# An expert stage's weights, gathers and order of work rewritten in a hybrid decoder layer

## The chip, the cores and the metric

The kernel runs on one core of one Trainium2 chip. The metric is the device time of one execution in microseconds (us), as the median of several runs. The engines are named as the profile names them: PE (TensorE, with PEld for its weight loads), DVE (VectorE), ACT (ScalarE), POOL (GpSimd) and SP (SyncE). Several engines can start DMAs, and all DMAs share the core's 16 DMA engines.

## The reference

One decoder layer over 4096 tokens of 1024 channels. A first sub-layer mixes tokens in four head groups and projects the result; the change doesn't touch its arithmetic. The second sub-layer is a mixture of 64 experts. Each token picks one group of eight experts and two experts in it.

```
hid = silu(xb @ w_gate[e]) * (xb @ w_up[e])     # xb: rows of the tokens of expert e, 1024 channels -> 256
y   = (hid @ w_down[e]) * g[:, None]            # 256 -> 1024, g: the token's gate for this expert
out = out.at[row_tok].add(y)                    # then x = x + gt_f * out, and a last rmsnorm
```

So 8192 pairs of token and expert are spread over 64 experts. With the inputs of the reference the counts by group of eight experts are:

```
 32  37  21  53  29  30  60  38
120 246 115 119 215 391 227 175
 44 147 213 198 114 101  97  82
191  98 206 152 121 138  91 137
 50 257 246 223 110 410 191 169
 62  96  55  58 126  63  26  46
 97  72  89 105 134  89  93  59
118 104 140 114 212 165 141 234
```

Everything is float32. Products use float32r operands, each number split into a high part and a low part, and three products stand for one.

## The kernel before

The layer runs in stages: `first`, `gdn`, `rwkv` (the mixers), `outp` (output projection, second norm, router), `moe` (the experts) and `final` (the last norm). `outp` writes the normed rows to `h2d` in DRAM and the sums to `acc`, and for each expert a list of (token, gate) to `lst`. Entries of a list that nobody takes name one of 128 extra rows past the tokens, with gate zero.

`moe` is one written-out loop over 64 experts. `manual_schedule` keeps each engine's instructions in the order of the program, and the framework adds the semaphores. The parts are:

- `moe_raw` (L1664) starts the loads of an expert's weights on SP into tiles `mraw` of 128x1024 (ten buffers): four tiles of gate|up, each filled by two loads of 256 KB (L1675, runs of 1 KB), and two tiles of down of 512 KB (L1679, runs of 4 KB).
- `moe_split` (L1683) splits a tile: ACT copies the high part (`mgh` or `mdh`, in `act`, L96), and L1688 subtracts it from the raw tile for the low part, on DVE for gate|up (`mgl`), on POOL for down (`mdl`).
- `gather` (L1749) is an indirect DMA on POOL: 128 rows of `h2d` by a list into `mxg`.
- `moe_t` (L1693) transposes 128 gathered rows on PE into PSUM (L1701); ACT and DVE write the two parts `mxh`, `mxl`.
- `moe_g` (L1707): 24 products of 512 columns (L1714 to L1716) give gate|up, then silu on ACT and the product on DVE give `hid`.
- `moe_ht` (L1720) transposes `hid` and splits it into `mhh`, `mhl`.
- `moe_d` (L1731): 12 products (L1741 to L1743), then DVE scales by the gate (L1744) into `my`, and POOL adds the rows to `acc` by an indirect DMA (L1745), which is called the scatter here.
- `count` (L1752) loads an expert's number of tokens into a register of every engine.

A block is 128 rows of one expert. In the loop over e the engines do: gather of the rows of e + 2; splits of gate|up of e + 1 and of down of e; products `moe_g` of e; hidden transposes of e - 1; transposes of the rows of e + 1; `moe_d` of e - 1. Then `If(n > 128)` (L1843) handles e's second block, and in it `If(n > 256)` (L1850) a hardware loop (L1851) over the rest, in which SP loads 128 list entries (`mix`) and POOL gathers the rows (`mxr`). At the end `fetch(e + 2)` starts the weights and, behind its own `If` (L1810), the gather of the second block of e + 2. What is left of an expert's last block (`pend`) is done in the turn of the next expert.

Of the kernel before, what the change touches and what calls it, by code (L numbers as in the profile page):

```python
# [8 lines left out]
F32 = mybir.dt.float32  # L9
# [10 lines left out]
D = 1024  # L20
# [21 lines left out]
class Trunk:  # L42
    """State shared by the stages of the kernel."""

    # when the steps of the two recurrent mixers come, in periods from the start of a superblock
# [17 lines left out]
    def __init__(self, ctx, tc, A, out, S=4096):  # L63
# [7 lines left out]
        # superblocks from which on the short convolution comes at the end of the two recurrent mixers  # L71
# [31 lines left out]
    # ------------------------------------------------------------------ constants  # L103
    def consts(self):
# [4 lines left out]
        def aff(name, shape, fill, keep, tests):  # L109
            """keep where every affine test (pattern, base, channel_multiplier, op) holds, else fill"""  # L110
# [8 lines left out]
        # two diagonal 64-blocks: of ones, and of ones where s <= t of [s, t]  # L119
# [10 lines left out]
    def parts(self, pool, x, bufs):  # L130
        """x [128, 2, 256] in two exact parts"""
# [18 lines left out]
    def col(self, pool, src, n, name):  # L150
        """a vector of n*128 numbers as [128, n] columns"""
# [4 lines left out]
    def row(self, pool, src, n, name):  # L156
        """a vector of n numbers on every partition"""
# [4 lines left out]
    def rsqrt_small(self, pool, x, eps, scale, tag):  # L162
        """(x*scale + eps)^-0.5 of a small tile: exp(-ln/2), then one Newton step"""
# [34 lines left out]
    def ada_step(self, pool, j, k, hp=None):  # L198
        """128 rows of part j of silu(c) @ ada_w, still to be summed over the partitions"""
# [14 lines left out]
    def ada_row(self, pool, psum, j, ptag):  # L214
        """part j of mod as a row in DRAM"""
# [36 lines left out]
    def h_norm(self, pool, t):  # L252
        """rows of tile t over their root mean square"""
# [16 lines left out]
    def h_make(self, pool, hp, psum, ptag, t, xs):  # L270
        """tile t of the modulated norm, channels on partitions, split in two float32r parts"""
# [18 lines left out]
    def h_load(self, hp, t, go=lambda f: f()):  # L290
        """superblock t, [128, TM] for each channel tile; go(f) runs each load"""
# [9 lines left out]
    def h_next(self, hp, t, gen):  # L301
        """the steps of gen; the loads of the superblock after the t-th go between them"""
# [10 lines left out]
    def fill_load(self, i, names, wp, hp, raw):  # L313
        """weights and the first tokens of the short convolution's i-th part"""
# [5 lines left out]
    def h_raw(self, hp):  # L320
        """room for 2048 numbers in the tiles of h_load"""
# [17 lines left out]
    def w_load(self, g, raw, n, src, c0, m=256, o=0):  # L339
        """m columns of src from c0 on to those of a group from o on; raw() is room for n numbers"""  # L340
# [1620 lines left out]
```

## Time and profile before

| | |
|---|---|
| time, median of 3 runs | 4150.07 us (4130.91 to 4164.19) |
| span of the profiled execution | 4143.8 us |
| PE, DVE, ACT, POOL busy, share of the span | 82%, 62%, 42%, 31% |
| DMA moved | 674.87 MB, mean 163 GB/s |
| experts' stage, from the first copy at L1830 on | 2788 to about 4040 us |

The shares are means over stages with different limits. Matmuls are pipelined and their ends are modelled, so a busy PE is not a PE at its peak. The page's DMA share is the mean busy share of the 16 DMA engines; it can pass 1 where packets overlap. PEclk is the granted share of TensorE's full clock.

### The profile page before, as it was taken

The page shows a single profiled execution, that of the slowest core. Times are in us where ns is not written, and L with a number is a line of the kernel's source. Part 1 is how long each engine was busy: PE and PEld are TensorE (multiplying, and loading weights), DVE is VectorE, ACT ScalarE, POOL GpSimd, SP SyncE. Part 2 cuts the span into 40 slices and gives each one's busy share as a digit, 9 for nine tenths or more (in the row PEclk, how much of TensorE's full clock was granted, in tenths as well). Part 3 has the DMA queues.
Part 4 walks back from the last instruction along what each step waited for, and adds up shares of the span by engine and source line. Part 5 has one row for each costly group of instructions (what it writes and reads, how often), then busy time and mean ns, then how long its engine had stood idle before and what let it go on. Part 6 is the DMA issues. An engine that isn't in the chain of part 4 may idle for free. (4 is left out here: it accounts for less than half of the span.)

```text
span 4143.8 us, 75906 instructions
## 1 busy us (share of the span) xinstructions
PE 3410.8 (82%) x28286; PEld 2886.0 (70%) x28286; DVE 2552.2 (62%) x6249; ACT 1740.9 (42%) x3235; POOL 1280.1 (31%) x1256
## 2 busy tenths in 40 slices
PE   5997778899999789999997999958758897588880
PEld 4786667888888678888886877846546675466660
DVE  6455557777776466777753665667535763278654
ACT  4233345655554245555432222226323552145533
POOL 1122221222221123433420112236424663256540
PEclk8999988989999899999998999979979998899995
DMA  8344452232234433333244544349747996489958
GB/s 301 120 174 148 166 169 76 76 99 77 78 96 120 128 93 81 84 106 83 80 126 155 180 139 146 122 147 323 220 143 203 301 284 168 114 267 341 298 151 331
DMA packets 555475, 674.87 MB, mean 163 GB/s; under 512 B 181921, under 2 KB 453561, under 8 KB 554977
## 3 DMA queue, kind: packets, MB, share of 16 engines
q1 hardware_dynamic: 500160, 482.78, 36.5%
q0 software_dynamic: 54816, 185.83, 15.7%
q8 instruction: 267, 4.37, 0.4%
q14 instruction: 232, 1.89, 0.1%
HBM read 487.37 MB, written 181.09 MB: 161 GB/s over the span
## 5 line engine op out<-in xcount | busy, mean ns | idle before, releaser
L1688 DVE TENSOR_TENSOR mgl<-mraw,mgh 128x1024 fp32r<-128x1024 f32 x256 | 403.2, 1616 | 54.3 <-ACT mgh L96 53.1
L1714 PE MATMUL mgu<-mgh,mxh 128*128 128x512 f32 x752 | 313.3, 417 | 92.3 <-PEq L1843 32.4
L96 ACT ACTIVATE mgh<-mraw 128x1024 fp32r<-128x1024 f32 x256 | 258.3, 1049 | 250.2 <-PEq L1843 118.6
L1688 POOL TENSOR_TENSOR mdl<-mraw,mdh 128x1024 fp32r<-128x1024 f32 x128 | 332.0, 2612 | 50.0 <-ACT mdh L96 48.2
L1715 PE MATMUL mgu<-mgl,mxh 128*128 128x512 f32 x752 | 303.3, 403 | 0.0
L1716 PE MATMUL mgu<-mgh,mxl 128*128 128x512 f32 x752 | 302.7, 402 | 0.0
L1714 PEld LDWEIGHTS mgu<-mgh,mxh 128*128 128x128 f32 x752 | 146.0, 194 | 154.0 <-issue 89.5
L1743 PE MATMUL mdn<-mdh,mhl 128*128 128x512 f32 x376 | 166.1, 442 | 77.8 <-DVE mhl L1728 77.8
L1744 DVE SCALAR_TENSOR_TENSOR my<-mdn,mpg,modr 128x512 f32<-128x512 f32 x178 | 133.5, 750 | 97.0 <-PE mdn L1743 95.3
L1741 PE MATMUL mdn<-mdh,mhh 128*128 128x512 f32 x376 | 169.3, 450 | 23.3 <-ACT mhh L96 23.1
L1704 DVE TENSOR_TENSOR mxl<-mtp,mxh 128x512 fp32r<-128x512 f32 x188 | 121.2, 683 | 89.1 <-ACT mxh L96 85.5
L1716 PEld LDWEIGHTS mgu<-mgh,mxl 128*128 128x128 f32 x752 | 145.2, 193 | 36.8 <-DVE mxl L1704 1.6
L1715 PEld LDWEIGHTS mgu<-mgl,mxh 128*128 128x128 f32 x752 | 146.4, 195 | 31.6
L1745 POOL DMA_INDIRECT acc<-my,mpt x64 | 104.9, 1639 | 185.4 <-DVEq L1843 96.6
L1742 PE MATMUL mdn<-mdl,mhh 128*128 128x512 f32 x376 | 160.5, 427 | 1.4 <-POOL mdl L1688 1.4
L82 ACT ACT_TABLE_LOAD x122 | 156.5, 1283 | 3.2 <-PEq L1947 0.8
L1743 PEld LDWEIGHTS mdn<-mdh,mhl 128*128 128x128 f32 x376 | 78.8, 210 | 112.7 <-DVE mhl L1728 92.9
L1749 POOL DMA_INDIRECT mxg<-h2d,ltok x89 | 121.4, 1364 | 113.1 <-DMA acc<-my,mpt 26.1
L1366 POOL TENSOR_TENSOR gSd<-gSb,gcd 128x256 f32<-128x256 f32 x64 | 54.6, 853 | 320.6 <-DVE gSb L1377 301.1
L96 ACT ACTIVATE mxh<-mtp 128x512 fp32r<-128x512 f32 x188 | 102.8, 597 | 102.9 <-PE mtp L1701 102.8
L96 ACT ACTIVATE mdh<-mraw 128x1024 fp32r<-128x1024 f32 x128 | 133.6, 1044 | 0.4 <-ACTq L1850 0.4
L96 ACT ACTIVATE mhid<-mgu 128x256 f32<-128x256 f32 x89 | 33.9, 381 | 231.0 <-PE mgu L1716 230.9
(559 smaller groups left out, 11242.0 us busy)
## 6 DMA issues: line engine op xcount, KB each, us to landing
mraw<-in_moe_w_gate_dram SPq DMA_DIRECT2D x256, 256.0 KB, 6.8
mraw<-in_moe_w_up_dram SPq DMA_DIRECT2D x256, 256.0 KB, 7.0
mraw<-in_moe_w_down_dram SPq DMA_DIRECT2D x128, 512.0 KB, 6.9
hhi<-hs_hi SPq DMA_DIRECT2D x168, 256.0 KB, 4.6
hlo<-hs_lo SPq DMA_DIRECT2D x168, 256.0 KB, 4.9
hx<-in_x_dram SPq DMA_DIRECT2D x32, 512.0 KB, 4.9
hs_hi<-hhi POOLq DMA_DIRECT2D x64, 256.0 KB, 7.4
hs_lo<-hlo POOLq DMA_DIRECT2D x64, 256.0 KB, 7.5
```

The costliest lines, as they stand in the source:

```text
L82: ld = self.nc.scalar.preload_act_table_set(name)
L96: i = self.nc.scalar.activation(out, in_, func, bias=bias, scale=scale, **kw)
L1688: eng.tensor_tensor(lo, raw, hi.bitcast(F32), op=ALU.subtract)
L1704: nc.vector.tensor_tensor(xl[:, s, :], ps, xh[:, s, :].bitcast(F32), op=ALU.subtract)
L1714: nc.tensor.matmul(ps, xh[:, k, :], gh[:, k, :], start=(k == 0), stop=False)
L1715: nc.tensor.matmul(ps, xh[:, k, :], gl[:, k, :], start=False, stop=False)
L1716: nc.tensor.matmul(ps, xl[:, k, :], gh[:, k, :], start=False, stop=(k == KT - 1))
L1741: nc.tensor.matmul(ps, hh[:, f, :], dh[:, f, s], start=(f == 0), stop=False)
L1742: nc.tensor.matmul(ps, hh[:, f, :], dl[:, f, s], start=False, stop=False)
L1743: nc.tensor.matmul(ps, hl[:, f, :], dh[:, f, s], start=False, stop=(f == 1))
L1744: nc.vector.scalar_tensor_tensor(y[:, s], ps, gate, self.gtf[:, s], op0=ALU.mult, op1=ALU.mult)
L1749: self.nc.gpsimd.indirect_dma_start(out=xg, out_offset=None, in_=self.h2d, in_offset=bass.IndirectOffsetOnAxis(ap=tok, axis=0))
```

## The change

Only the experts' stage and what feeds it are changed.

- An expert's 1024 input channels are dealt to partitions as (p k) and no longer as (k p), so that a partition's rows of gate or up lie together: four loads of 512 KB in runs of 4 KB in place of eight of 256 KB. The second norm writes its rows in the matching order of channels (strided write), and the shift row (part 3) and the router's weights are loaded in that order.
- Down of expert e is loaded with gate|up of e + 1.
- Gathers have a bounds check: entries past the tokens are left out, and `h2d` has no extra rows. Tiles that are gathered into are cleared once.
- The lists of all experts are held for 512 entries, token and gate side by side.
- The order of an expert's work: the hidden transposes of e - 1 stand in the middle of `moe_g` of e; the splits of gate|up of e + 1 lie two before and two behind; down's splits come after them, the second one half on POOL and half on DVE.
- The second block's gather (`fetch_more`) is issued for every expert, at the end of the expert before, without an `If`. Blocks 3 and 4 are nested straight code, and the hardware loop is left for more than 512 rows.

```diff
@@ ada_row
-        nc.sync.dma_start(self.modd[j:j + 1], row[0:1])
+        if j == 3:
+            nc.sync.dma_start(self.modd[j:j + 1].rearrange("o (k q) -> o q k", k=KT),
+                              row[0:1].rearrange("o (q k) -> o q k", k=KT))
+        else:
+            nc.sync.dma_start(self.modd[j:j + 1], row[0:1])
...
@@ out_dense
-        V.scalar_tensor_tensor(y, x, r, self.scf, op0=ALU.mult, op1=ALU.mult)
+        swap = lambda a: a.rearrange("p (q k) -> p q k", k=KT)
+        V.scalar_tensor_tensor(y.rearrange("p (k q) -> p q k", k=KT), swap(x), r, swap(self.scf), op0=ALU.mult,
+                               op1=ALU.mult)
...
@@ moe_raw
+        room = lambda: rp.tile([128, 1024], F32, name="mraw", tag="mraw", bufs=10)
+        g, d = [], []
+        if e < 64:
+            for h in range(2):
+                for n in ("moe_w_gate", "moe_w_up"):
+                    g.append(room())
+                    nc.sync.dma_start(g[-1].rearrange("p (k n) -> p k n", k=4),
+                                      A[n][0, e].rearrange("(p k) n -> p k n", p=128)[:, 4 * h:4 * h + 4, :])
+        if e > 0:
+            for f in range(2):
+                d.append(room())
+                nc.sync.dma_start(d[-1], A["moe_w_down"][0, e - 1][f * 128:f * 128 + 128, :])
+        return g, d
...
@@ moe_split_d
+        self.act(hi, raw, AF.Copy)
+        for eng, s in ([(nc.gpsimd, slice(0, D))] if f == 0 else [(nc.gpsimd, slice(0, 512)), (nc.vector, slice(512, D))]):
+            eng.tensor_tensor(lo[:, s], raw[:, s], hi[:, s].bitcast(F32), op=ALU.subtract)
...
@@ moe_g
         for k in range(KT):
+            if mid is not None and k == KT // 2:
+                mid()
...
@@ gather
         self.nc.gpsimd.indirect_dma_start(out=xg, out_offset=None, in_=self.h2d,
-                                          in_offset=bass.IndirectOffsetOnAxis(ap=tok, axis=0))
+                                          in_offset=bass.IndirectOffsetOnAxis(ap=tg[:, 0:1], axis=0),
+                                          bounds_check=self.S - 1, oob_is_err=False)
...
@@ moe
+            more = [pool.tile([128, D], F32, name=f"mxg{i}") for i in range(2)]
...
+            def fetch_more(e):
+                if e < 64:
+                    self.gather(more[0], tg[:, 1, e])
...
+            def turn(pend):
+                return self.moe_ht(pool, psum, pend[0], "mh")
...
                     fetch_x(e + 2)
-                    for k in range(4):
-                        split_g(e + 1, k)
-                        if k % 2:
-                            split_d(e, k // 2)
-                    self.moe_g(psum, wg[e], x, hid)
-                    if pend is not None:
-                        h = self.moe_ht(pool, psum, pend[0], "mh")
-                    x = make_x(e + 1)
+                    split_g(e + 1, 0)
+                    split_g(e + 1, 1)
+                    h = []
+                    ps = self.moe_g(psum, wg[e], x, mid=lambda: h.append(turn(pend)) if pend else None)
+                    split_g(e + 1, 2)
+                    split_g(e + 1, 3)
+                    split_d(e, 0)
+                    self.moe_h(ps, hid)
+                    x = make_x(e + 1)
+                    split_d(e, 1)
+                    n = self.count(ci[0:1, e:e + 1])
                     if pend is not None:
-                        self.moe_d(pool, psum, wd[e - 1], h, pend[1], pend[2], "my", 2)
+                        self.moe_d(pool, psum, wd[e - 1], h[0], pend[1], "my", 2)
                     with tc.If(n > 128):
+                        self.gather(more[1], tg[:, 2, e])
                         h = self.moe_ht(pool, psum, hid, "mi")
-                        x1 = self.moe_t(pool, psum, xgs[e, 1], "mu", 1)
-                        self.moe_d(pool, psum, wd[e], h, tok[:, 0, e:e + 1], pg, "mv", 1)
...
+                        x1 = self.moe_t(pool, psum, more[0], "mu", 1)
+                        self.moe_d(pool, psum, wd[e], h, tg[:, 0, e], "mv", 1)
+                        V.tensor_copy(pt, tg[:, 1, e])
+                        self.moe_h(self.moe_g(psum, wg[e], x1, "igu"), hid)
                         with tc.If(n > 256):
...
+                            self.gather(more[0], tg[:, 3, e])
+                            x1 = self.moe_t(pool, psum, more[1], "mu", 1)
+                            h = self.moe_ht(pool, psum, hid, "mi")
+                            V.tensor_copy(pt, tg[:, 2, e])
+                            self.moe_h(self.moe_g(psum, wg[e], x1), hid)
+                            self.moe_d(pool, psum, wd[e], h, tg[:, 1, e], "mv", 1)
+                            with tc.If(n > 384):
+                                x1 = self.moe_t(pool, psum, more[0], "mu", 1)
+                                h = self.moe_ht(pool, psum, hid, "mi")
+                                V.tensor_copy(pt, tg[:, 3, e])
+                                self.moe_h(self.moe_g(psum, wg[e], x1, "igu"), hid)
+                                self.moe_d(pool, psum, wd[e], h, tg[:, 2, e], "mv", 1)
+                                with tc.If(n > 512):
+                                    with tc.For_i(512, n, 128) as i:
...
+                    fetch_more(e + 1)
                     fetch(e + 2)
```

## Rows read from the trace of the kernel before

**Rows 1.** Windows: start:end, length, then busy us by engine, PEclk, DMA share, GB/s.
```profile
2788.00:2898.00 110.00, 90.67 (x402) 70.32 (x402) 85.45 (x106) 68.59 (x91) 68.84 (x35) 0.93 1.02 323
...
3251.00:3409.00 158.00, 145.76 (x692) 115.63 (x692) 105.39 (x160) 84.36 (x121) 100.44 (x51) 1.00 0.97 294
...
3670.00:3780.00 110.00, 89.02 (x405) 67.76 (x404) 95.70 (x106) 66.62 (x90) 76.96 (x35) 0.98 1.02 323
3780.00:3902.00 122.00, 102.72 (x465) 80.27 (x466) 89.61 (x119) 69.76 (x95) 78.66 (x40) 0.96 1.03 321
...
4060.00:4143.00 83.00, 0.00 (x0) 0.00 (x0) 42.47 (x66) 30.86 (x66) 0.00 (x0) 0.50 0.91 354
```

**Rows 2.** Groups by line: count, busy us, mean ns, idle before and what ended it.
```profile
L1714 PE MATMUL mgu<-mgh,mxh 128*128 128x512 f32 x752 | 313.3, 417 | 92.3 <-PEq L1843 32.4 <-ACTq L1850 17.3 <-PEq L1754 9.2
...
L1749 POOL DMA_INDIRECT mxg<-h2d,ltok x89 | 121.4, 1364 | 113.1 <-DMA acc<-my,mpt 26.1 <-issue 25.2 <-DVE mpg L1831 13.3
```

**Rows 3.** Timeline of PE: start us, us, instruction, idle before it; two neighbouring experts.
```profile
3851.02 0.50 PE L1714 MATMUL mgu<-mgh,mxh 128*128 128x512 f32 x1 [0.86 <-PEq L1843]
...
3861.59 0.50 PE L1714 MATMUL mgu<-mgh,mxh 128*128 128x512 f32 x1 [0.87 <-PEq L1843]
```

**Rows 4.** Windows of experts 33 and 13 and of the one after 13.
```profile
3409.00:3462.00 53.00, 31.86 (x138) 24.41 (x136) 16.51 (x26) 9.99 (x17) 16.75 (x10) 0.84 0.42 100
...
2975.00:3061.00 86.00, 43.65 (x184) 33.27 (x182) 19.54 (x33) 12.70 (x22) 16.92 (x11) 0.79 0.29 56
3061.00:3092.00 31.00, 23.59 (x95) 18.73 (x96) 12.31 (x21) 10.04 (x15) 9.95 (x6) 0.81 0.88 288
```

**Rows 5.** Waits of the experts' stage: total us, times, longest.
```profile
PEld mdn L1743 <- DVE mhl L1728: 92.9, 44, 5.3
...
PE mtp L1701 <- DMA mxr<-h2d,mix: 72.2, 5, 19.0
```

**Rows 6.** Timeline of POOL: two scatters of neighbouring one-block experts.
```profile
3708.39 1.57 POOL L1745 DMA_INDIRECT acc<-my,mpt  x1 [2.10 <-DVEq L1843]
...
3720.29 1.57 POOL L1745 DMA_INDIRECT acc<-my,mpt  x1 [2.10 <-DVEq L1843]
```

**Rows 7.** Timelines of DVE, POOL and PE in expert 19.
```profile
3186.75 6.43 DVE L1688 TENSOR_TENSOR mgl<-mraw,mgh 128x1024 fp32r<-128x1024 f32 x2 [0.19 <-ACT mgh L96]
...
3185.86 6.25 POOL L1688 TENSOR_TENSOR mdl<-mraw,mdh 128x1024 fp32r<-128x1024 f32 x2 [1.48 <-ACT mdh L96]
...
3193.91 0.80 PE L1743 MATMUL mdn<-mdh,mhl 128*128 128x512 f32 x1 [3.86 <-DVE mhl L1728]
3194.50 0.63 PE L1741 MATMUL mdn<-mdh,mhh 128*128 128x512 f32 x1
3194.93 0.63 PE L1742 MATMUL mdn<-mdl,mhh 128*128 128x512 f32 x1
```

**Rows 8.** The page's DMA issues: count, KB each, us from issue to landing.
```profile
mraw<-in_moe_w_gate_dram SPq DMA_DIRECT2D x256, 256.0 KB, 6.8
...
mraw<-in_moe_w_down_dram SPq DMA_DIRECT2D x128, 512.0 KB, 6.9
```

**Rows 9.** Instructions by tile and line: ns min/median/max; landings of L1745, us.
```profile
L96 ACT ACTIVATE mgh<-mraw x256: 1038/1045/1065, 2761.0 to 3991.6; 128x1024 fp32r<-128x1024 f32 x128
L1688 DVE TENSOR_TENSOR mgl<-mraw,mgh x256: 1210/1226/6335, 2779.0 to 3994.5; 128x1024 fp32r<-128x1024 f32 x128
...
L1688 POOL TENSOR_TENSOR mdl<-mraw,mdh x128: 2338/2434/3426, 2790.1 to 4017.6; 128x1024 fp32r<-128x1024 f32 x128
...
L1749 POOL DMA_INDIRECT mxg<-h2d,ltok x89: 941/1314/2054, 2778.6 to 3989.7; - x89
...
L1745 POOL DMA_INDIRECT acc<-my,mpt x64: 1555/1582/2409, 2813.4 to 4040.9; - x64
...
DMA to landing us min/median/max: 6.0/7.6/10.1
```

**Rows 10.** Waits of SP's DMA queue in the experts' stage.
```profile
SPq L1675 <- DMA mraw<-in_moe_w_up_dram: 37.7, 74, 2.1
```

**Rows 11.** Instructions of the second norm's tile: ns min/median/max.
```profile
L1621 DVE SCALAR_TENSOR_TENSOR oy<-ox,orr,modr x32: 1278/1284/1286, 2292.5 to 2742.3; 128x1024 f32<-128x1024 f32 x32
```

**Rows 12.** Windows: a stretch of the output projection's stage.
```profile
2300.00:2500.00 200.00, 192.39 (x1031) 161.76 (x1030) 125.73 (x348) 54.94 (x116) 38.95 (x49) 0.98 0.42 142
```

More of the change, by code (lines that the diff above doesn't have):

```diff
@@ L1432, in out_room @@
         nc, S = self.nc, self.S
-        self.h2d = self.dram.tile([S + 128, D], F32, name="h2d")
+        self.h2d = self.dram.tile([S, D], F32, name="h2d")
         self.acc = self.dram.tile([S + 128, D], F32, name="acc")
@@ L1436, in out_room @@
         nc.vector.memset(z, 0.0)
-        for x in (self.h2d, self.acc):
+        for x in (self.acc,):
             nc.gpsimd.dma_start(x[S:S + 128, :].rearrange("p (a b) -> p a b", b=256),
@@ L1705, in moe_t, with moe_g @@
         return xh, xl
-    def moe_g(self, psum, w, x, hid, tag="mgu"):
+    def moe_g(self, psum, w, x, tag="mgu", mid=None):
         nc = self.nc
@@ L1729, in moe_ht, with moe_d @@
         return hh, hl
-    def moe_d(self, pool, psum, w, h, tok, gate, tag, bufs):
+    def moe_d(self, pool, psum, w, h, tg, tag, bufs):
         nc = self.nc
@@ L1759, in moe_lists @@
         nc, S = self.nc, self.S
[L1760 to L1773 removed]
+        raw = pool.tile([64, 512, 2], I32, name="lraw", tag="mv")
+        nc.gpsimd.dma_start(raw, self.lst.rearrange("(e s) c -> e s c", s=S)[:, 0:512, :])
+        tf = pool.tile([64, 2, 512], F32, name="ltg", tag="muh")
+        nc.vector.tensor_copy(tf[:, 0, :], raw[:, :, 0])
+        nc.vector.tensor_copy(tf[:, 1, :], raw.bitcast(F32)[:, :, 1])
+        tg = pool.tile([128, 4, 64, 2], I32, name="ltg")
+        for j, out in enumerate((tg, tg.bitcast(F32))):
+            ps = psum.tile([128, 4, 64], F32, name="lps", tag="mt")
+            for b in range(4):
+                nc.tensor.transpose(ps[:, b, :], tf[:, j, b * 128:b * 128 + 128], self.ident[0:64, 0:64])
+            nc.vector.tensor_copy(out[:, :, :, j], ps)
+        return tg
     def moe(self):
@@ L1783, in moe, with split_g, split_d @@
             V.tensor_copy(ci, self.cnt)
-            tok, gate = self.moe_lists(pool, psum)
+            tg = self.moe_lists(pool, psum)
             self.use_set(SILU)
-            wg, wd, raws, xgs, ns = {}, {}, {}, {}, {}
-            def split_g(e, k):
+            wg, wd, raws, xgs = {}, {}, {}, {}
+            more = [pool.tile([128, D], F32, name=f"mxg{i}") for i in range(2)]
+            for x in more:
+                nc.gpsimd.memset(x, 0.0)
+            def split_g(e, j):
                 if e < 64:
-                    if k == 0:
+                    if j == 0:
                         wg[e] = self.moe_w(wp, "mg", KT, 512)
-                    self.moe_split(V, wg[e], raws[e][k], 2 * k, 2)
-            def split_d(e, k):
-                if k == 0:
+                    self.moe_split_g(wg[e], raws[e][0][j], j)
+            def split_d(e, f):
+                if f == 0:
                     wd[e] = self.moe_w(wp, "md", 2, D)
-                self.moe_split(nc.gpsimd, wd[e], raws[e][4 + k], k, 1)
+                self.moe_split_d(wd[e], raws[e + 1][1][f], f)
             def fetch_x(e):
@@ L1801, in fetch_x @@
                     xgs[e] = pool.tile([128, D], F32, name="mxg", tag="mxg", bufs=2)
-                    self.gather(xgs[e], tok[:, 0, e:e + 1])
+                    if e < 2:
+                        nc.gpsimd.memset(xgs[e], 0.0)
+                    self.gather(xgs[e], tg[:, 0, e])
+            def fetch_more(e):
+                if e < 64:
+                    self.gather(more[0], tg[:, 1, e])
             def fetch(e):
-                if e < 64:
+                if e < 65:
                     raws[e] = self.moe_raw(rp, e)
-                    xgs[e, 1] = pool.tile([128, D], F32, name="mxg1", tag="mxg1", bufs=2)
-                    ns[e] = self.count(ci[0:1, e:e + 1])
-                    with tc.If(ns[e] > 128):
-                        self.gather(xgs[e, 1], tok[:, 1, e:e + 1])
             def make_x(e):
                 return self.moe_t(pool, psum, xgs[e], "mx", 2) if e < 64 else None
+            def turn(pend):
+                return self.moe_ht(pool, psum, pend[0], "mh")
             with tc.manual_schedule(engines=ENGINES):
@@ L1819, in moe @@
                 fetch_x(1)
-                for k in range(4):
-                    split_g(0, k)
+                fetch_more(0)
+                for j in range(4):
+                    split_g(0, j)
                 x = make_x(0)
@@ L1832, in moe @@
+                    V.tensor_copy(pt, tg[:, 0, e])
                     fetch_x(e + 2)
-                    for k in range(4):
-                        split_g(e + 1, k)
-                        if k % 2:
-                            split_d(e, k // 2)
-                    self.moe_g(psum, wg[e], x, hid)
+                    split_g(e + 1, 0)
+                    split_g(e + 1, 1)
+                    h = []
+                    ps = self.moe_g(psum, wg[e], x, mid=lambda: h.append(turn(pend)) if pend else None)
```

88 lines of the change are left out of this document (30 added, 58 removed).

## The prediction, made before the run

> **What bounds the kernel now.** I first cut the experts' stage into stretches [rows 1]. It runs from 2788 us, where expert 0's tokens are copied (L1830), to 4040 us: 1252 us. The instruction counts give its size [rows 2]: 752 matmuls of L1714, eight to a block, are 94 blocks of 128 rows. There are 64 first blocks, 89 - 64 = 25 second ones, and 5 turns of the loop at L1851. By the reference's routing 39 experts have one block, 22 two, and experts 33, 13 and 37 (257, 391, 410 rows) three, four and four.
>
> The stretch 3251 to 3409 is undisturbed: granted clock 1.00 (the 2.4 GHz level), five experts of one block and five of two, 15 blocks in 158 us, 10.55 us each [rows 1]. TensorE sets that pace. Two first matmuls of neighbouring one-block experts lie 3861.59 - 3851.02 = 10.57 us apart, 0.87 of it the branch at L1843 [rows 3]. At it 94 blocks take 992 us, so 260 us are lost. They lie in three places.
>
> Loops: 86 and 53 us for experts 13 and 33, 31 for the one after 13 [rows 4]; expert 37 and the two other followers are alike (87, 32, 30). 319 us for 17 blocks, which at 10.55 are 179. 140 lost. TensorE waits 72 us for rows that are gathered only inside the loop [rows 5], and SyncE sits in the loop, so the next weights start late.
>
> Full DMA: in 2788:2898, 3670:3780 and 3780:3902 the DMA share is 1.02 to 1.03. They hold 26 one-block experts and one of two: 342 us for 28 blocks, against 295. 47 lost. The scatters of two such experts lie 3720.29 - 3708.39 = 11.90 us apart [rows 6].
>
> The rest: 1252 - 319 - 342 - 158 = 433 us for 34 blocks, against 359. 74 lost. Here the chain of one stall reads [rows 7]: two gate|up subtractions on VectorE (L1688) take 6.43 us in place of 2.4 while GpSimd does its two; so the low part of the hidden rows (mhl) is late, and TensorE stands 3.86 us before L1743, then works at the lower clock, 10 matmuls 0.43 us apart and not 0.23 as at the 2.4 GHz level. TensorE's sequencer waits 93 us for mhl in all, 44 times [rows 5].
>
> **Loops to straight code.** Removed: the list load on SyncE, the late gather, the barriers of the loop, SyncE's stay in it. A straight block costs 10.55 plus about 1 us, since its transposes need PSUM and the x tile that the block before still uses. Five blocks and three branches: +8. Nothing of SyncE is left in a body that runs here (over 512 rows none), so the next weights flow under the long expert. -140 + 8 = -132; if SyncE is still late, each of three restarts keeps up to 10: -102.
>
> **Runs of 4 KB, empty entries skipped.** Gate and up, 2.1 MB an expert, came in 1 KB runs. The last norm moves 4 KB rows at 354 GB/s with a share of 0.91, 389 at a full one; the full stretches, mixed, give 323/1.02 = 317 [rows 1]. 2.1 MB take 5.4 us at the one and 6.6 at the other: between 0 and 1.2 saved, and I take 0.9, for a down load of 512 KB lands as soon (6.9 us) as a gate load of 256 (6.8) [rows 8]. The expert groups that fill these stretches have 37, 66 and 81 rows of 128, so a gather moves 0.35, 0.24 or 0.19 MB less: 0.6 to 1.1 us at 317 GB/s. 11.9 falls to about 10.3, under TensorE's 10.55: -47 (-20 if half comes through). GpSimd still issues every gather, 39 more than before, since the second block's is now unconditional.
>
> **Order of an expert.** The hidden transposes go into the middle of the gate|up products, down's splits behind the four gate|up splits. VectorE's fourth subtraction is released one ScalarE copy (1.05 us) ahead of GpSimd's first, and lasts 1.2 [rows 9]: they hardly meet, and mhl stands before them. Of the 74 us I take 55, between 74 and 20. Added on VectorE: 512 columns of down, half of 1.23 = 0.6 us an expert. Its busy share in the full stretches is 0.73 to 0.87 [rows 1]; against the shorter expert it stays below one, and TensorE hides it.
> [...]
>
> **Small edits.** The second norm's permuted write, the router's rows, one 1024-element store of a modulation row, longer lists (four transposes more, a 256 KB load): the norm's 32 instructions of 1.28 us [rows 11] lie beside products that keep TensorE busy 192 us of 200 [rows 12], and cost nothing there; were they twice as long and bare, 41 us. The store runs once, stages before its row is read. The longer lists add 0 to 5 us before the first expert. I take 2.
>
> So far: -132 - 47 - 55 + 2 = -232.
>
> **The wait that is added.** fetch_more(e + 1) is issued by GpSimd at the end of expert e, behind the scatter of expert e - 1. In the records each software transfer names the semaphore that its landing raises. No view prints them, so this stands without a row: eight in turn, in program order, skipped bodies counted, and a transfer is issued only when the last on its semaphore has landed. SyncE's loads show such waits for earlier landings [rows 10]. Before, an expert has six (L1749 twice, L1745 twice, and two in the loop). After, it has ten: fetch_x, the scatter of e - 1, seven in the nested body, fetch_more. Places two and ten are eight apart: fetch_more waits for the scatter just issued. Behind it GpSimd holds the next fetch_x, both subtractions of down, and the next scatter, which needs them only by its place in the queue. One round of a one-block expert is then: landing of the scatter, 6.0 at best and 7.6 in the median, I take 7.4 as the DMA is less full; two gathers of 1.31; 2.43 for one subtraction, 1.2 for the half; and an allowance of 0.3 for branch and count [rows 9]: 7.4 + 2.6 + 2.4 + 1.2 + 0.3 = 13.9 us. That is 3.35 over 10.55, and 39 experts give +131. In an expert of two blocks the round is hidden, but 12 of them follow one of one block and their second rows come late; TensorE runs ahead by an expert at most and pays there. 1 us each for what is not in the rounds: +12. Behind such stands the clock falls as in [rows 7]: 10 matmuls of 0.2 us, some 2 us for half of the 12, +12. Together +155; with landings of 6.0 it is +100, with 8.4 +194.
>
> **Sum.** -232 + 155 = -77 against the profiled span of 4143.8: 4067. The span lies 6 us under the median of 4150.07, within the spread of the three runs (4130.91 to 4164.19), and what lies around it has no row; I forecast for the median and round to 4070. With every term at its good end (-140, -47, -74, +2, +100) it is 3991, with every one at its bad end (-102, -20, -20, +5, +194) 4207. They are not met together; the landing, the largest, alone moves it from 4018 to 4112, and with a little of the others I give the forecast 4005 to 4130 of its own.
>
> **Rivals.**
> Untied: fetch_more finds its semaphore free, because the numbering at the branches is another. GpSimd's work of 2.6 + 2.4 + 1.2 + 1.6 = 7.8 us then fits into 10.55, and the whole -232 stays: 3918. For it: nothing in the views says that the count goes on over skipped bodies. Against: in the records consecutive scatters are six places apart. [...]
>
> Long gathers, the slower one: the bounds check, or a list of nothing but empty entries, makes a gather on GpSimd longer than 1.31. Two stand in each round, 39 rounds: 78 us for each us. From 2.3 us on the gain is gone (77/78 = 1.0 us more), from 2.9 the kernel is over 1% slower; at 3.5 us it is 4070 + 171 = 4240. For it: no gather with a check is in the trace, and durations already vary from 0.94 to 2.05 [rows 9]. Against: the 128 entries of a list are walked either way,.
>
> Not skipped: the empty entries are moved all the same. Then each of 39 experts moves 0.5 MB more, the DMA stays full, landings are at 8.4 and -47 goes: 4070 + 39 + 47 = 4156, no change.
>
> **Chances.** The forecast 0.66, untied 0.20, long gathers 0.08, not skipped 0.06. A measurement here tells 1% (41 us) from no change at best. Under 4109: untied, and nine tenths of the forecast, 0.80. Within 1%: most of the rest of the forecast and the unskipped, 0.12. Slower 0.08. The range goes from 3910, which takes in untied, to 4130, the bound of the forecast.
>
> **What would show it.** Scatters (L1745's line) of one-block experts near 14 us apart, with the gather of fetch_more right behind a landing, in 3670 to 3780's experts; 10.6 apart shows untied. No transposes waiting for mxr; experts of four blocks near 44 us; 4 KB loads and a DMA share under 0.9; VectorE subtractions of 1.2 us throughout. If GpSimd's gathers last over 2 us, or if TensorE waits for the second rows in experts of two blocks by more than 12 us, the sum is wrong.

## The result

The changed kernel takes 4011.9 us (median of four runs, 4007.4 to 4025.9), the kernel before 4140.5 beside it on the same chip: a ratio of 0.969, 95% interval 0.965 to 0.973. The forecast was 4070, with a range of 3910 to 4130. The profiled span went from 4143.8 to 4012.1 us, 131.7 less; the sum had said 77.

### The profile page after: what moved, and what is told of

The parts are those of the page before. It is cut to its first block, busy times and chain, and to the rows that moved or that the text cites. A ratio compares the mean times of both kernels' runs of the same rounds, so it can differ in the third digit from the quotient of the medians.

```text
span 4012.1 us, 75052 instructions
## 1 busy us (share of the span) xinstructions
PE 3390.5 (85%) x28290; PEld 2880.4 (72%) x28290; DVE 2536.2 (63%) x6229; ACT 1733.2 (43%) x3235; POOL 1282.7 (32%) x1321
## 5 line engine op out<-in xcount | busy, mean ns | idle before, releaser
L1734 PE MATMUL mgu<-mgh,mxh 128*128 128x512 f32 x752 | 327.7, 436 | 122.4 <-PEq L1877 80.7
L1698 DVE TENSOR_TENSOR mgl<-mraw,mgh 128x1024 fp32r<-128x1024 f32 x256 | 302.5, 1224 | 100.3 <-ACT mgh L96 98.6
L1706 POOL TENSOR_TENSOR mdl<-mraw,mdh 128x1024 fp32r<-128x1024 f32 (+1 forms) x128 | 277.8, 2190 | 164.3 <-ACT mdh L96 163.7
L1775 POOL DMA_INDIRECT mxg<-h2d,ltg x156 | 184.1, 1180 | 113.0 <-issue 58.7
L1765 PE MATMUL mdn<-mdh,mhh 128*128 128x512 f32 x376 | 155.6, 414 | 0.9 <-ACT mhh L96 0.9
L1767 PE MATMUL mdn<-mdh,mhl 128*128 128x512 f32 x376 | 149.8, 398 | 6.5 <-DVE mhl L1752 6.5
L1766 PE MATMUL mdn<-mdl,mhh 128*128 128x512 f32 x376 | 147.9, 393 | 0.0
L1742 DVE TENSOR_TENSOR mhid<-mhid,mgu 128x256 f32<-128x256 f32 x94 | 39.2, 417 | 156.4 <-ACT mhid L96 85.0
L1610 PE MATMUL ops<-wo0h,ohi 128*128 128x512 f32 x256 | 107.0, 418 | 27.6 <-ACT ohi L96 27.6
L1719 PE MATMUL mtp<-ident,mxg 128*128 128x128 f32 x752 | 98.7, 275 | 25.4 <-DMA mxg<-h2d,ltg 22.1
```

What stands on the lines that cost most here:

```text
L1698: self.nc.vector.tensor_tensor(lo, raw, hi.bitcast(F32), op=ALU.subtract)
L1706: eng.tensor_tensor(lo[:, s], raw[:, s], hi[:, s].bitcast(F32), op=ALU.subtract)
L1734: nc.tensor.matmul(ps, xh[:, k, :], gh[:, k, :], start=(k == 0), stop=False)
L1765: nc.tensor.matmul(ps, hh[:, f, :], dh[:, f, s], start=(f == 0), stop=False)
L1766: nc.tensor.matmul(ps, hh[:, f, :], dl[:, f, s], start=False, stop=False)
L1767: nc.tensor.matmul(ps, hl[:, f, :], dh[:, f, s], start=False, stop=(f == 1))
```

## The profile after

The first view cuts the changed kernel into stretches, to be read as [rows 1]: the experts' stage from the first copy of a list to the last product, experts 1 to 9 (all of one block but the last), expert 13 with four blocks, eleven one-block experts in a row, and the last norm.

```profile
2804.00:3905.00 1101.00, 955.93 (x4306) 756.99 (x4306) 696.91 (x969) 526.54 (x755) 604.61 (x373) 0.95 0.85 254
2812.00:2938.00 126.00, 104.37 (x461) 83.00 (x462) 87.83 (x117) 69.41 (x95) 78.28 (x48) 0.93 0.96 303
2986.00:3029.00 43.00, 39.74 (x185) 31.04 (x186) 20.26 (x34) 13.37 (x23) 14.27 (x10) 1.00 0.61 161
3549.00:3697.00 148.00, 121.44 (x506) 95.88 (x506) 102.24 (x133) 81.73 (x110) 92.11 (x56) 0.88 0.98 302
3905.00:4012.00 107.00, 2.68 (x9) 1.82 (x7) 46.75 (x74) 38.93 (x80) 1.57 (x1) 0.52 0.85 324
```

The stage is 1101 us against 1252, 151 less, but it begins 16 us later, 23 if counted from the norm's first tile. Expert 13 went from 86 us [rows 4] to 43. The row that does not fit is the fourth: 148 us for eleven one-block experts, 13.45 us each, where the same experts took 12.2 before (most of them 11.9 [rows 6]). That is nearly the 13.9 of my forecast, and the reason I gave for it is not there. This is GpSimd's timeline of the changed kernel in that run of experts:

```profile
3628.89 1.62 POOL L1770 DMA_INDIRECT acc<-my,mpt  x1 [0.48 <-DVEq L1877]
3631.36 1.03 POOL L1775 DMA_INDIRECT mxg<-h2d,ltg  x1 [0.85 <-issue]
3632.70 1.93 POOL L1775 DMA_INDIRECT mxg<-h2d,ltg  x1 [0.30 <-issue]
3638.35 4.36 POOL L1706 TENSOR_TENSOR mdl<-mraw,mdh 128x1024 fp32r<-128x1024 f32 x2 [3.72 <-ACT mdh L96]
```

The scatter is issued at 3628.89 and the gather of second rows 2.5 us later, while scatters here land 8.5 us after their issue. The gather waits for no landing, and GpSimd stands 3.72 us in front of its subtractions. It is so in all 38 one-block experts that have a scatter ahead of this gather: it is issued 1.9 to 5.8 us behind it. The records, which name the semaphore that each landing raises, show why: there are eight in turn (110 to 117), the scatter at 3628.89 has 114, and the gather 117, three places on and not eight as I had counted. So it is in all 38, and the transfer that had the gather's semaphore last was issued at least 14.9 us before, while neither scatter nor gather lands later than 12.0 us after its issue.

What stands is TensorE. Its waits from expert 1 on in the changed kernel (total us, times, longest; PEq and DVEq are the parts of TensorE and VectorE that pass branches and waits, their sequencers):

```profile
PE mgu L1734 <- PEq L1877: 80.7, 30, 4.1
PE mgu L1734 <- DVEq L1884: 23.4, 21, 1.2
PE mtp L1719 <- DMA mxg<-h2d,ltg: 10.8, 10, 2.5
PE mgu L1734 <- DVE mpt L1862: 9.4, 5, 2.0
```

The largest names its own sequencer at L1877, the branch over the body of an expert with more than 128 rows. That line's instructions, in the changed kernel (ns min/median/max):

```profile
L1877 PEldq COMPARE_BRANCH  x64: 65/5115/7353, 2807.0 to 3886.0; - x64
L1877 ACTq COMPARE_BRANCH  x64: 34/45/55, 2810.4 to 3887.9; - x64
L1877 POOLq COMPARE_BRANCH  x64: 34/45/53, 2812.0 to 3892.2; - x64
L1877 DVEq COMPARE_BRANCH  x64: 43/56/67, 2812.1 to 3890.3; - x64
...
L1877 POOLq INC_SWDGE_SEM  x39: 635/1147/1883, 2812.5 to 3816.5; - x39
```

and the same branch in the kernel before, at L1843:

```profile
L1843 PEldq COMPARE_BRANCH  x64: 65/336/2792, 2791.0 to 4021.0; - x64
```

TensorE's branch went from a median of 0.34 us to 5.1. In the records of single instructions all 39 taken ones of the changed kernel last 4.3 to 7.4 us, and all 25 that fall through less than 0.1; inside each of the 39 lies exactly one 16 KB packet of the queue for instructions, which in the median starts 3.1 us into the branch and ends 1.5 us ahead of its end. Before, two of 64 were over 1 us, one of them with such a packet. The timeline of TensorE at one of the 39 shows how much is hidden, and three windows there (gap, first products, the rest of the expert) the granted clock:

```profile
3641.04 0.39 PE L1767 MATMUL mdn<-mdh,mhl 128*128 128x512 f32 x1
3643.89 0.77 PE L1734 MATMUL mgu<-mgh,mxh 128*128 128x512 f32 x1 [2.46 <-PEq L1877]
3644.46 0.63 PE L1735 MATMUL mgu<-mgl,mxh 128*128 128x512 f32 x1
```
```profile
3641.43:3643.89 2.46, 0.00 (x1) 0.03 (x1) 1.65 (x4) 0.22 (x1) 1.98 (x2) 0.94 0.95 338
3643.89:3647.00 3.11, 3.10 (x7) 2.45 (x8) 2.24 (x2) 1.79 (x2) 2.49 (x2) 0.50 1.09 205
3647.00:3655.00 8.00, 8.00 (x40) 6.28 (x38) 5.37 (x8) 5.42 (x8) 4.07 (x3) 1.00 0.96 301
```

The branch began at 3637.89 and ended at 3643.52, 5.6 us. The products queued ahead of it ran until 3641.43, so 3.5 us are covered and TensorE stands 2.46. Then seven products run at a granted clock of 0.50, 0.43 us apart and not 0.23: 1.4 us more. Of the 14.3 us of this expert, 2.46 + 1.4 = 3.9 are lost so. In 38 of the 39 experts 3.53 to 3.56 us of the branch are covered, 2.74 in the first, and TensorE stands 1.7 to 4.1 us, 2.47 in the mean; before the change it stood 0.92 there.

Two rows of the second norm's tile (L1628, L1630) and the subtractions of the splits, in the changed kernel, each to be read as in [rows 9, 11]:

```profile
L1628 DVE SCALAR_TENSOR_TENSOR oy<-ox,orr,modr x32: 1956/2022/2078, 2285.6 to 2749.3; 128x1024 f32<-128x1024 f32 x32
L1630 DVE TENSOR_TENSOR oy<-oy,modr x32: 1224/1225/1257, 2287.8 to 2751.3; 128x1024 f32<-128x1024 f32 x32
```
```profile
L1698 DVE TENSOR_TENSOR mgl<-mraw,mgh x256: 1210/1224/1286, 2788.4 to 3866.5; 128x1024 fp32r<-128x1024 f32 x128
```

The write with swapped channels takes 2.02 us, not 1.28. The 32 tiles now need 463.7 us from first to last, not 449.8 [rows 11], so 14 of the 32 x 0.74 = 24 us come through. And the stretched gate|up subtractions on VectorE are gone: 1286 ns at most, where it was 6335 [rows 9].

## The experiments

Twelve kernels, each an edit of the changed one, timed in three rounds beside the kernel before. Ratios are to that, whose median lay between 4127 and 4142 us, so that 10 or 15 us between two kernels of different rounds tell nothing by themselves. The other columns are from the profiled execution: the time between the first copies (L1862) of neighbouring experts, summed over the 39 experts of one block, 20 of two blocks (up to expert 61), and the three of three or four; and TensorE's branches over n > 128 that last over 1 us, of 39 taken. All but at most two of these in a kernel hold a 16 KB packet of code.

The expectations weigh three theories of the 13.45 us. Code: TensorE's branch jumps to code that has still to be fetched. Round: GpSimd's queue of scatter, gathers and subtractions sets the pace, as I forecast. DMA: the full transfers set it.

| kernel | median us | ratio, 95% interval | 39 of one | 20 of two | three large | long branches |
|---|---|---|---|---|---|---|
| before | 4140.5 | 1 | 484.0 | 490.3 | 226.3 | 2 |
| changed | 4011.9 | 0.969 (0.965 to 0.973) | 488.6 | 446.6 | 121.8 | 39 |
| a_no_over512 | 4016.2 | 0.971 (0.965 to 0.978) | 477.3 | 464.4 | 124.8 | 14 |
| a_loops | 4085.5 | 0.989 (0.983 to 0.995) | 431.1 | 487.3 | 213.3 | 3 |
| a_more_known | 4009.0 | 0.972 (0.965 to 0.978) | 482.4 | 446.9 | 121.5 | 38 |
| a_scatter_skip | 4000.4 | 0.968 (0.962 to 0.974) | 479.7 | 437.4 | 122.8 | 39 |
| a_igu | 4009.6 | 0.970 (0.967 to 0.974) | 477.3 | 450.4 | 121.6 | 38 |
| a_igu_no512 | 3999.0 | 0.967 (0.964 to 0.970) | 453.9 | 473.2 | 121.2 | 16 |
| a_oldorder | 4210.4 | 1.019 (1.015 to 1.024) | 614.5 | 504.2 | 131.6 | 39 |
| a_plain_1k | 3985.0 | 0.965 (0.961 to 0.969) | 473.1 | 438.4 | 124.4 | 39 |
| a_stride_t | 3997.9 | 0.966 (0.962 to 0.971) | 483.7 | 446.2 | 123.2 | 39 |
| a_noskip | 4053.4 | 0.979 (0.971 to 0.987) | 508.2 | 468.3 | 126.5 | 39 |
| a_best | 3950.9 | 0.953 (0.948 to 0.958) | 449.7 | 441.8 | 117.5 | 15 |
| a_best_xmid | 3951.9 | 0.955 (0.950 to 0.959) | 453.4 | 442.1 | 115.6 | 20 |

**The forecast's wait, taken away.**

```diff
 def fetch_more(e):
-    if e < 64:
+    if e in (9, 12, 13, 14, 15, 17, ...):    # the 25 experts with second rows
```

> The changed kernel with the gather of the second rows issued only for the 25 experts that have second rows (written into the program by hand, which holds for these inputs only). Round, as I forecast it, with the gather of second rows tied to a landing: 39 x 3.35 = 131 off, 3880; the gather's own 1.2 us alone: 39 x 1.2 = 47 off, 3965. Code and DMA: the 128 skipped entries are packets of 9 ns, no change, 4012 within 10.

4009: no change. 39 gathers on GpSimd, and whatever they waited for, cost nothing that can be told. The round that I forecast does not set the pace.

**Blocks 3 and 4 back in a loop.** Under the second branch the two nested blocks and the loop from 512 become one `For_i(256, n, 128)` that loads its list and gathers its rows, as before; the early gather into more[1] goes.

> The changed kernel with blocks 3 and 4 of experts 13, 33 and 37 in the loop as it was before; all else as changed. Code: the jump is over two blocks again, one-block experts come to 11 us (39 x 2.4 = 94 off), and the loops bring back 132: 4050. Round and DMA: one-block experts stay at 13.4, 4012 + 132 = 4144.

Its branch (ns min/median/max):

```profile
L1877 PEldq COMPARE_BRANCH  x64: 65/335/6409, 2805.1 to 3957.6; - x64
```

The long branches fall from 39 to 3 and the one-block experts from 488.6 to 431.1 us, 11.05 each. The other experts take 487.3 + 213.3 against 446.6 + 121.8: 132 more. GpSimd's work, the order and the loads of one-block experts are those of the changed kernel. So the straight code gives 132 us in the experts that run it, and takes 57 back where it is jumped over. Of the 132, 111 lie in the three large experts and the three behind them. The other 21 lie in experts of two blocks; TensorE waits 51.7 us for gathered rows in this kernel and 10.8 in the changed one. The code theory's 132 came, but 57 and not its 94, so that the time is 4085 and not 4050. Nor are the 57 the fetch alone: the loop writes its products into igu, the PSUM tile of block 2, and not into that of the first block; what that is worth comes out in the next two parts.

**A shorter body, by itself.** The loop for rows past 512 is left out (no expert has so many), so that a taken branch jumps over three blocks.

> The changed kernel without the loop for rows past 512 (no expert has so many), so that TensorE's branch over the body of a one-block expert jumps over three blocks of straight code and not four. Three theories of why one-block experts take 13.4 us in runs. Code: the jump over four blocks ends in code that has still to be fetched, TensorE stands 2 to 3 us before each next expert and then works some products at the lower clock; the jump over three blocks (the branch at n > 256 in two-block experts) costs 1.1 us. Then 39 x (1.4 us of gap + 1 us of clock) = 94 us go: about 3920, one-block experts near 11.2. Round: GpSimd's order (scatter, two gathers, two subtractions) sets the pace: no change, 4012. DMA: the full transfers set it: no change, 4012.

The long branches fall to 14 of 39 (13 of them with a packet), as the code theory wants, and the time stays: 4016, not 3920. In their place TensorE waits for VectorE, and more for gathered rows:

```profile
PE mgu L1734 <- DVEq L1877: 58.9, 27, 4.1
PE mtp L1719 <- DMA mxg<-h2d,ltg: 36.4, 17, 6.4
PE mgu L1734 <- PEq L1877: 24.9, 9, 3.1
```

How it waits for VectorE, the changed kernel itself shows at an expert whose branch lasts 4.94 us and ends at 3589.93 (TensorE's timeline, then VectorE's):

```profile
3588.17 0.39 PE L1767 MATMUL mdn<-mdh,mhl 128*128 128x512 f32 x1
3590.25 0.48 PE L1734 MATMUL mgu<-mgh,mxh 128*128 128x512 f32 x1 [1.70 <-DVE mpt L1862]
```
```profile
3587.54 1.04 DVE L1706 TENSOR_TENSOR mdl<-mraw,mdh 128x512 fp32r<-128x512 f32 x1 [0.20 <-issue]
3588.51 1.40 DVE L1768 SCALAR_TENSOR_TENSOR my<-mdn,mpt,modr 128x512 f32<-128x512 f32 x2
3590.05 0.17 DVE L1862 COPY mpt<-ltg 128x2 int32<-128x2 int32 x1
```

TensorE's products are done at 3588.56 and its next stands until VectorE has finished both multiplications at 3589.91. In the records VectorE then, at 3589.95, raises its semaphore (100) by an instruction of L1877 that only the 39 experts that skip the body have, and TensorE's first product, at 3590.25, waits for that semaphore. A body that is skipped can matter to it since block 3 (L1889) writes its gate|up product into the PSUM tile of the first block; the next edit tests this. The two causes lie side by side, and whichever is later shows: in the changed kernel no stand of TensorE at this branch is shorter than the 1.70 us here.

**The PSUM tile, alone and together.**

```diff
-self.moe_h(self.moe_g(psum, wg[e], x1), hid)           # block 3
+self.moe_h(self.moe_g(psum, wg[e], x1, "igu"), hid)
```

> The changed kernel with the gate|up products of block 3 in the PSUM tile of block 2 (igu) and not in that of the first block (mgu). PSUM theory: since a body that is skipped writes mgu, TensorE's first product behind the branch waits until VectorE has passed its own branch, and VectorE passes it only behind its last multiplication for the expert before; without that the stand of 1.08 us behind the second branch falls to the 0.53 us of the run with loops (25 x 0.55 = 14), and behind the first branch the stand stays where code is fetched (39 x 5.6 us, of which 3.5 lie under queued products): 3995. Rival, that the branch itself costs the 1.1 and 1.7 us: no change, 4012 within 8.

> Both: block 3 in igu, and no loop for rows past 512 (none has so many). In the run without that loop only 14 of 39 taken branches fetched code (39 in the changed kernel), and VectorE's passage took the place of the fetch. Code and PSUM theory: the mean stand before a one-block expert falls from 2.03 to about 1 us (39), some 80 products at the lower clock go (16), 14 from the two-block experts: 4012 - 69 = 3943. DMA theory: runs of one-block experts can't fall below the 12.0 us that the packets of one take, so that at most half comes: 3980.

Alone it gives nothing that can be measured (4010), though the stand behind the second branch is halved, from the 23.4 us above in 21 waits to 11.5:

```profile
PE mgu L1734 <- ACTq L1884: 11.5, 21, 0.6
```

Together the one-block experts fall by 35 us to 11.6 each, under the 12.0 at which the DMA theory stops them. In the 23 of them with a short branch TensorE stands 0.30 us each; without the change of tile it stood 1.3 to 4.1 us in the 25 with a short branch. This shows the tile to be what the wait for VectorE came from. But the experts of two blocks take 27 us more, and the time is 3999, not 3943. TensorE's waits in that kernel's stage:

```profile
PE mtp L1719 <- DMA mxg<-h2d,ltg: 51.9, 16, 9.7
PE mgu L1734 <- PEq L1877: 36.6, 18, 3.8
```

TensorE waited 10.8 us for gathered rows in the changed kernel and waits 51.9 here. The longest of these waits stand ahead of second rows: they are gathered at the end of the expert before, and a faster one-block expert leaves their landing uncovered. Of the 27 us, 20 lie in the ten experts of two blocks that follow one of one. The gain of one kind of expert is paid by the next. My prediction put this wait at 1 us for 12 experts; it is no more than that in the changed kernel (10.8 us for all gathered rows), but not here.

**The order as before.** All six splits come ahead of the products, both low halves of down go to GpSimd, and the hidden transposes behind the products.

> The changed kernel with the order of an expert as before: all six splits ahead of the gate|up products, both low halves of down on GpSimd, the hidden transposes behind the products. Forecast term: the new order is worth 55 (20 to 74), so 4012 + 55 = 4067, with VectorE's subtractions stretched to 1.8 us or more and TensorE waiting for mhl again. Rival: the new order is worth nothing, since what it freed is lost at the branch: 4012 within 10.

4210: the order is worth 198 us here, not 55, and without it the change would have made the kernel slower than before. TensorE's waits:

```profile
PE mgu L1734 <- PEq L1875: 124.9, 36, 5.1
PE mdn L1767 <- DVE mhl L1752: 108.9, 48, 4.6
```

mhl is late again, 48 times; in the changed kernel these waits are 6.5 us. A wait for mhl also stops TensorE's sequencer ahead of the branch, so less work is queued over it: 2.5 us of it are covered in the median, not 3.5, and the branch shows 124.9 us, not 80.7. So of the 198 us the waits for mhl make 102 and those at the branch 44; the rest was not traced.

**Runs, swap and skip.** First, gate and up in runs of 1 KB and every row plain:

```diff
-A[n][0, e].rearrange("(p k) n -> p k n", p=128)
+A[n][0, e].rearrange("(k p) n -> p k n", p=128)
-V.scalar_tensor_tensor(y.rearrange("p (k q) -> p q k", k=KT), swap(x), r, swap(self.scf), ...)
+V.scalar_tensor_tensor(y, x, r, self.scf, ...)
```

> The changed kernel without the 4 KB runs and all that they need: gate and up come in runs of 1 KB again (the same six loads of 512 KB), the norm writes its rows plainly, and the router's rows and the modulation row are as before. The norm's 32 instructions of 2.02 us are 1.28 us again: 14 to 24 off. The loads take 0.5 us more of full DMA for each expert by their packets (49 ns for 1 KB, 180 for 4 KB). If DMA sets the pace of one-block experts: 39 x 0.5 = 20 on, sum near 4012; if my term of 20 to 47 holds: 4018 to 4050; if TensorE's branch sets it: 4012 - 14 = 3998.

Then the runs of 4 KB without the swap, its work done by the transposes of gathered rows:

```diff
-nc.tensor.transpose(ps[:, k, :], xg[:, (4 * g + k) * 128:(4 * g + k + 1) * 128], self.ident)
+nc.tensor.transpose(ps[:, k, :], xg.rearrange("p (q k) -> p k q", k=KT)[:, 4 * g + k, :], self.ident)
```

> The changed kernel with the 4 KB runs kept, but the swap of channels that they need taken out of the norm: the norm, the router's rows and the modulation row are plain again, and the transposes of gathered rows read every eighth column instead. Beside the run with plain rows and 1 KB runs (3985) this tells the runs from the swap. If the norm's write is the whole loss and 4 KB runs help the loads by 0.4 to 0.5 us an expert: 3965 to 3985. If the 4 KB runs themselves do harm (one-block experts at 12.5 as in the changed kernel, and the first expert's weights ahead of its rows): 3998 and more. If TensorE reads a stride of 32 bytes slower, the 752 transposes of 0.11 us show it: twice as long is 83 more.

And gathers that move the empty entries, without the bounds check:

> The changed kernel with gathers that move the empty entries too (into rows of zeros behind the others, as before). A one-block expert then moves some 57 rows more with its first gather and 128 more with the gather of second rows: 185 packets of 160 ns on 16 engines, 1.85 us of transfers. If transfers set the pace of its one-block experts: 39 x 1.85 = 72, 4084. If TensorE's branch sets it: its code packets and rows only land a little later, 4012 to 4030. My forecast gave the unskipped case 86 more than the skipped one.

Without 4 KB runs the kernel takes 3985, 27 less by the medians and 16 by the ratios, whose intervals overlap. Both plain kernels have the norm's instruction at 1.28 us. From the norm's first tile to the first copy of a list it is 495.2 us before the change, 518.2 after, and 500.4 and 505.5 in these two: the swap costs 13 to 18 us, the longer lists with what lies around them 5 to 10. With the swap gone, 4 KB runs (3998) are no better than 1 KB runs (3985); the intervals overlap. The transposes' reads with a stride take no longer as products (275 ns, 272 before), their weight loads 193 ns, not 140. Moving the empty entries costs 41 us (4053), 20 of it in the one-block experts. That lies between the two numbers expected, 4084 if transfers set the pace and 4012 to 4030 if the branch does; some 11 of the 20 us are a longer stand of TensorE at the branch, which lasts 5.9 us in the mean of the long ones and not 5.65.

**Scatters that skip the empty entries too.** The same bounds check on the scatter.

> The changed kernel with scatters that skip the empty entries as the gathers do. A scattered row takes 328 ns of one of 16 engines, and a one-block expert has some 56 empty entries: 1.15 us of full DMA less. DMA: 39 x 1.15 = 45 off, 3967. Code: no change in TensorE's stand before the next expert, 4012 within 10. Round, tied to a landing: landings come some 1 us sooner, 3975; not tied: 4012.

4000, by its ratio no change that can be told. Some 1.1 us of transfers less in each one-block expert move them by 0.23 us. So full transfers alone don't set their pace, though the DMA share was 0.98 in the changed kernel.

**What they point to, together.** Plain rows, 1 KB runs, the scatter's check, block 3 in igu, and rows past 512 in a pass behind all experts, so that the body has three blocks.

> What the runs so far point to, together: plain rows and 1 KB runs (27 off), scatters that skip empty entries (12), block 3 in igu and no code for rows past 512 in an expert's body (13): these rows get a pass of their own behind all experts, which one branch skips here. If the gains add: 4012 - 52 = 3960. If they are the same time twice (each frees transfers or a wait that another then ends): 3980.

> The same, and the transposes of the next expert's rows go into the middle of the gate|up products, behind the hidden transposes, so that 20 long products and not 12 and eight short transposes are queued on TensorE when its sequencer reaches the branch. Code theory: the work behind the branch grows from 3.5 to 4.5 us, each fetch of 5.6 shows 1.1 us less; with some 16 fetches and a lower clock behind each, 25 off: 3935. Rival: what limits the sequencer's lead is not the number of queued instructions but a wait, and the transposes now stand for rows or PSUM in the middle of the products: no change, or some 20 on.

The second has one edit more:

```diff
-ps = self.moe_g(psum, wg[e], x, mid=lambda: h.append(turn(pend)) if pend else None)
+def mid():
+    if pend:
+        h.append(turn(pend))
+    nx.append(make_x(e + 1))
+ps = self.moe_g(psum, wg[e], x, mid=mid)
...
-x = make_x(e + 1)
+x = nx[0]
```

3951 and 3952: faster than both kernels, 0.953 of the one before. The gains add: 61 us by the medians, where 52 were expected (3960). The longer queue does at its place what the code theory says: waits at TensorE's own branch fall from 21.5 us to 10.1, with more long branches (20, not 15). But the time stays, for its transposes now wait for rows. The waits of a_best from expert 1 on, then those of a_best_xmid:

```profile
PE mtp L1712 <- DMA mxg<-h2d,ltg: 38.2, 15, 4.5
PE mgu L1727 <- PEq L1871: 21.5, 27, 3.3
```
```profile
PE mtp L1712 <- DMA mxg<-h2d,ltg: 53.7, 30, 4.9
PE mdn L1760 <- DVE mhl L1745: 13.7, 13, 1.4
PE mgu L1727 <- PEq L1876: 10.1, 15, 1.4
```

What both wait for most now is the landing of rows.

## Why the prediction was right and where it failed

The direction, the range and the size of the loops were right. The step that failed is the wait that is added: fetch_more was to wait for the landing of the scatter just issued, +155 us. It does not: its semaphore lies three places from the scatter's and not eight, so the seven transfers of the skipped body don't count as I took them, and leaving the gather out changes nothing. One-block experts took 13.45 us in runs all the same, close to the 13.9 of that step, from a cause that no step or rival named. That the forecast came near is luck: 155 us of waiting did not come, and neither did 100 of the 232 us of gains.

- **Loops to straight code**, -132: shown. The three large experts and the three behind them took 319 us before; by this term they were to take 187, and they take 188. With the loops back they take 299, so that 111 us are the loops' own and the other 20 come with the other edits. The step's other half was missing: "five blocks and three branches: +8" priced the branches that run and left out the 39 that jump. They cost 57 us, by the long branch with its packet of code, the wait for VectorE's semaphore and the lower clock (0.50) behind the stand. The net is 74 (4085.5 to 4011.9). The stand at the branch was 0.87 us [rows 3], and I took it as fixed whatever lies behind it; over four blocks of straight code it is 1.7 to 4.1.
- **4 KB runs and skip**, -47: the skip is worth 41, the runs nothing that can be told. My 0.9 us an expert came from full DMA as the bound; TensorE's branch had become it. The rival "not skipped" had the size of the skip at 86.
- **Order**, -55: the mechanism was right (subtractions at 1.2 us throughout, hardly a wait for mhl), the term far too small. Beside straight code the order is worth 198: 102 are waits for mhl, and 44 come from the branch, over which it queues work. Beside loops it was not measured alone; there the one-block experts fell from 484 to 431 us, by 53, with the skip in it.
- **Small edits**, +2: mis-sized. I wrote that the norm "lies beside products that keep TensorE busy" and costs nothing; 14 of its 24 us came through, and with the lists the start is some 23 us later. The bound of 41 held.
- **The halves of down** overlap in time in all 64 experts of the changed kernel. VectorE's half lasts 0.69 us at best, 1.04 in the median and 4.52 at worst, where I took 0.6. GpSimd's half lasts 1.7 us in the mean, 1.27 at best, and the sum had 1.2: some 0.5 us more. But GpSimd stands ahead of its subtractions (3.72 us above), so these 0.5 us are not seen.
- **The rivals.** Untied was right in its mechanism, the numbering, and 94 us off in its time, since the branch took what the gather left. Long gathers: they last 1.03 us in the median, refuted. Not skipped: refuted, since moving the empty entries costs 41 us.
- **Small slips in the working.** A gather of 37 rows in 128 moves 0.37 MB less, not 0.35. The 12 experts whose second rows follow a one-block expert are ten of two blocks, and experts 33 and 37. The forecast starts from the span, the ends of its range and the rivals from the median, 6 us more. What the working calls the 2.4 GHz level is in the traces a granted clock of 1.00, with products 0.23 us apart; at 0.50 they are 0.43 apart. None of these changes the outcome.
- **What would show it:** of the signs I named, no waits for mxr, four blocks in 44 us (42.7 and 45.3) and 1.2 us on VectorE came. A DMA share under 0.9 did not: it is 0.98 in the eleven one-block experts. Scatters 14 us apart came too, and they had been meant as proof. The gather right behind a landing, the sign that told the causes apart, did not come.

## What to carry to other kernels

Straight code in a body that is often skipped is paid for by those who skip it (57 us here): count the instructions that the busiest engine jumps over, read that engine's own branch in the trace, and ask how much work is queued ahead of it. An engine that skipped a body was still waited for here on account of a tile that the body would have written (1.3 to 4.1 us at a short branch, 0.30 without that tile), so keep the tiles of a rare body apart from those that the next iteration needs first. And a forecast period that comes true shows nothing about its cause: name beforehand the row that only your mechanism can produce.

## What the runs showed of the hardware

- A taken branch of TensorE with one 16 KB packet of code inside, of some 1 us, lasts 4.3 to 7.4 us in the changed kernel. Over four blocks of 46 products each, 39 of 39 had such a packet; over three, 13 to 18 in four kernels; over two, 3 (a_loops) and 1 (before). In the kernel before, 37 of 39 taken branches last 0.34 us in the median and 0.86 at most. No other engine's branch in the changed kernel's stage was over 0.07 us.
- Of such a branch 3.5 us are hidden under products already queued (3.53 to 3.56 in 38 of 39 experts), so that 1.7 to 4.1 show. With eight short transposes moved out of that queue, so that long products stand in their place, TensorE's waits there fall from 21.5 us (a_best) to 10.1 in all (a_best_xmid).
- In the 39 experts that skip the body, VectorE raises its semaphore 0.04 us in the median (0.17 at most) behind the end of its own last instruction ahead of the branch. Where TensorE waited for that it stood 1.3 to 4.1 us at a short branch (a_no_over512), and 0.30 where no skipped body wrote its next PSUM tile (a_igu_no512).
- In the same 39 experts GpSimd has an instruction of its own (INC_SWDGE_SEM, 1.15 us in the median), at whose end seven of the eight semaphores of its transfers are raised; it lay in slack here.
